# MLP down projections of a two-layer trunk kernel: activations as the stationary operand, weights as the moving one

## The chip, the cores and the metric

The kernel runs on one core of a Trainium2 chip. The metric is the time of one execution on the device in microseconds (us), as the median of several runs. The profile is one further execution, taken by the hardware profiler. PE is the matrix engine (TensorE), PEld its weight loads, DVE the vector engine, ACT the scalar engine, POOL GpSimd, and SP the queue from which the loads are issued.

## The reference

A trunk of two layers over 256 tokens with 2048 features, all in float32. Each layer has a mixing part (layer 0: an RWKV-7 recurrence, layer 1: attention with forget gates) and an MLP with 8192 hidden features:

```python
def rms_norm(x, gain):
    y = x * lax.rsqrt(jnp.mean(x * x, axis=-1, keepdims=True) + RMS_EPS)
    return y * gain

def squared_relu_mlp(h, w_up, w_down):
    return jnp.square(jax.nn.relu(h @ w_up)) @ w_down
...
for layer in range(DEPTH):            # DEPTH = 2
    x = x + mixed                     # RWKV-7 or attention
    x = x + squared_relu_mlp(rms_norm(x, ffn_norm[layer]), mlp_w_up[layer], mlp_w_down[layer])
return rms_norm(x, final_norm)
```

The change touches `squared_relu_mlp` alone, and in it the product with `w_down` (8192 x 2048 in each layer).

## The kernel before

**Layout.** The stream `xT` lies in SBUF with features on the partitions: 16 blocks (KT) of 128 features, each 128 x 256 tokens. Every float32 operand is kept as two parts, a rounded high part and the rest (`h` and `lo` of a weight, `[:, k, 0, :]` and `[:, k, 1, :]` of an activation in `opA` and `opB`), and a product is high x high + high x rest + rest x high.

**Weights.** `load_split` (line 194) loads a piece of a weight matrix into a raw buffer (`wr`) from SP. ACT casts it to the high part (`wh`, line 204), and DVE subtracts that from the raw piece (`wl`, line 206). In the MLP a raw piece is WK = 4 blocks of 128 rows by 512 columns (1024 KB), split two blocks at a time. The raw and split buffers have pools of their own there, three buffers of each kind (WRAW, WSP). Elsewhere pieces of 512 KB run through the global pool `wraw` with four buffers.

**The MLP.** `mlp` (line 346) goes through four chunks (c) of 2048 hidden features. In each chunk there are four up groups (g), each giving 512 hidden features, and four down groups, each adding to 512 features of `xT`. Both kinds of group use `gemm_wide` (line 241). For each of the 16 blocks k and each of the four 128-column parts of the weights, a part of the weight is stationary and the activations move. A 512-wide matmul (line 254) takes the high weight with both activation parts side by side, and a 256-wide one (line 256) takes the rest of the weight with the high activations. So one block takes eight matmuls, and the four PSUM banks of a group are taken in turn from two pools of four banks (`psm`, `pss`). At the end of a group ACT copies the second half of each bank (line 261) and DVE adds the first half to it (line 262).

**After a down group** DVE multiplies by `r2`, the square of the RMS factor (line 363, one value per token, laid along the free dimension), and POOL adds the result to `xT` (line 366; DVE for the last group of a layer). `r2` is made once in each layer, after the first up group: `norm.ln()` sums the squares over the partitions with matmuls against ones (`nps`, line 324) and takes the logarithm on ACT (line 326), and `norm.power` the exponential (line 330). In the last chunk `final` follows each pair of blocks: squares for the next norm and the operands of the next stage (`after0`, `after1`).

**Order.** The order in which each engine takes its instructions is settled when the program is built, and is not simply that of the code: casts and subtractions for coming pieces stand ahead of the evictions of a finished group.

The stage that computes the attention's values (lines 924 to 938) already has the form to which the change turns the down groups: activations stationary, 512 weight columns moving, two banks for the two halves of the tokens, and the factor per token as a scalar per partition. Ahead of it two transposes (line 922) turn that factor round.

## Time and profile before

| what | us |
|---|---|
| median of 3 runs | 2569.55 (2557.32 to 2569.76) |
| the profiled execution, its own time | 2563.87 |
| its span, first to last instruction | 2562.1 |

The span is what the profile's rows are measured in; 1.8 us of the profiled execution's time lie around it. A row of a group of instructions gives line, engine, operation, output<-inputs, count, busy time and mean duration of one; a row of the timeline gives the start, the duration and the instruction, and in brackets how long its engine had been idle and what ended that.

### The profile page before, as it was taken

The numbers are of one execution on the slowest core, as the hardware profiler recorded it, in microseconds if no ns is written. First come the engines' busy times: TensorE is split into PE (matmuls) and PEld (weight loads), VectorE is DVE, ScalarE is ACT, GpSimd is POOL, SyncE is SP. The second block draws the span as 40 slices with busy tenths as digits, with TensorE's granted clock in tenths as the row PEclk, the third lists the DMA queues.
The fourth block names the chain that finished last, engine by engine and source line by source line (L and its number), as shares of the span: only waits on it lengthen the run. The fifth ranks groups of instructions, "written<-read, shape, count | busy, mean of one in ns | idle before, by whom it ended". The sixth has DMA issues, their size and how long they took to land. (4 is left out here: it accounts for less than half of the span.)

```text
span 2562.1 us, 47095 instructions
## 1 busy us (share of the span) xinstructions
PE 2474.4 (97%) x19102; PEld 2208.3 (86%) x19102; DVE 1620.4 (63%) x2266; ACT 1272.2 (50%) x2098; POOL 526.2 (21%) x428
## 2 busy tenths in 40 slices
PE   6889999999999999999999999999999999999997
PEld 4889988888888888888888898999988888888886
DVE  8987557776755555555556655677555555555555
ACT  3655435454555454454455544455454454554454
POOL 5444324332311211111112100010011112111112
PEclk9999999999999999999999999999999999999998
DMA  4668856555765555555556366546455555556553
GB/s 149 199 201 246 249 180 189 161 166 159 237 202 189 182 181 197 182 189 188 181 181 197 97 183 196 181 158 198 149 190 184 194 187 191 183 195 194 186 195 116
DMA packets 279641, 472.88 MB, mean 185 GB/s; under 512 B 52464, under 2 KB 62976, under 8 KB 279424
## 3 DMA queue, kind: packets, MB, share of 16 engines
q1 hardware_dynamic: 279424, 469.89, 57.9%
q8 instruction: 149, 2.44, 0.4%
q14 instruction: 68, 0.56, 0.1%
HBM read 445.70 MB, written 24.13 MB: 183 GB/s over the span
## 5 line engine op out<-in xcount | busy, mean ns | idle before, releaser
L206 DVE TENSOR_TENSOR wl<-wr,wh 128x1024 fp32r<-128x1024 f32 (+1 forms) x960 | 965.9, 1010 | 740.9 <-ACT wh L204 735.7
L204 ACT CAST wh<-wr 128x1024 fp32r<-128x1024 f32 (+1 forms) x969 | 815.8, 846 | 909.7 <-PE mmw L254 595.0
L254 PE MATMUL mmw<-opB,wh 128*128 128x512 f32 x2048 | 717.4, 397 | 4.9 <-DVE xT L850 4.9
L254 PE MATMUL mmw<-opA,wh 128*128 128x512 f32 x2048 | 718.0, 397 | 0.2 <-ACT wh L204 0.2
L256 PE MATMUL mmw<-opA,wl 128*128 128x256 f32 x2048 | 572.5, 280 | 0.9 <-DVE wl L206 0.9
L256 PE MATMUL mmw<-opB,wl 128*128 128x256 f32 x2048 | 571.7, 279 | 0.0
L254 PEld LDWEIGHTS mmw<-opB,wh 128*128 128x128 f32 x2048 | 384.9, 188 | 97.4 <-DVE xT L850 5.1
L254 PEld LDWEIGHTS mmw<-opA,wh 128*128 128x128 f32 x2048 | 384.9, 188 | 93.0 <-ACT wh L204 0.5
L256 PEld LDWEIGHTS mmw<-opA,wl 128*128 128x128 f32 x2048 | 386.5, 189 | 1.4 <-DVE wl L206 1.3
L256 PEld LDWEIGHTS mmw<-opB,wl 128*128 128x128 f32 x2048 | 386.4, 189 | 0.2
L212 PE MATMUL mm<-opB,wh 128*128 128x256 f32 x1024 | 304.0, 297 | 1.2 <-DVE wh L202 1.2
L214 PE MATMUL mm<-opB,wl 128*128 128x256 f32 x1024 | 294.7, 288 | 7.0 <-DVE wl L206 4.8
L213 PE MATMUL mm<-opB,wh 128*128 128x256 f32 x1024 | 294.6, 288 | 3.9 <-DVE opB L343 3.8
L366 POOL TENSOR_TENSOR xT<-xT,mt 128x512 f32<-128x512 f32 x60 | 128.8, 2147 | 533.8 <-DVE mt L363 533.8
L212 PE MATMUL mm<-opA,wh 128*128 128x256 f32 x768 | 227.7, 297 | 0.0
L214 PE MATMUL mm<-opA,wl 128*128 128x256 f32 x768 | 218.5, 285 | 2.7 <-POOL wl L206 1.5
L213 PE MATMUL mm<-opA,wh 128*128 128x256 f32 x768 | 218.8, 285 | 0.0
L353 POOL TENSOR_TENSOR ms<-mt 128x512 f32<-128x512 f32 x64 | 81.1, 1267 | 636.5 <-ACT mt L351 636.5
L214 PEld LDWEIGHTS mm<-opB,wl 128*128 128x128 f32 x1024 | 198.4, 194 | 9.2 <-DVE wl L206 5.6
L213 PEld LDWEIGHTS mm<-opB,wh 128*128 128x128 f32 x1024 | 198.4, 194 | 7.5 <-DVE opB L343 5.7
L212 PEld LDWEIGHTS mm<-opB,wh 128*128 128x128 f32 x1024 | 198.2, 194 | 5.4 <-DVE wh L202 1.4
L214 PEld LDWEIGHTS mm<-opA,wl 128*128 128x128 f32 x768 | 147.5, 192 | 3.7 <-POOL wl L206 1.7
(252 smaller groups left out, 2711.0 us busy)
## 6 DMA issues: line engine op xcount, KB each, us to landing
wr<-in_mlp_w_up_dram SPq DMA_DIRECT2D x128, 1024.0 KB, 5.4
wr<-in_mlp_w_down_dram SPq DMA_DIRECT2D x128, 1024.0 KB, 5.0
wr<-in_w_rkv_dram SPq DMA_DIRECT2D x96, 512.0 KB, 4.7
wr<-in_w_kvf_dram SPq DMA_DIRECT2D x64, 512.0 KB, 3.7
wr<-in_w_o_dram SPq DMA_DIRECT2D x32, 512.0 KB, 4.0
wr<-in_fox_w_q_dram SPq DMA_DIRECT2D x32, 512.0 KB, 3.8
wr<-in_fox_w_o_dram SPq DMA_DIRECT2D x32, 512.0 KB, 4.0
s_bk<-bk SPq DMA_DIRECT2D x8, 512.0 KB, 3.0
```

Of the source, the lines that this page charges most:

```text
L204: nc.scalar.copy(h, raw[:, k:k + per, :])
L206: (G if share["l"] and c % share["l"] == 0 else V).tensor_tensor(lo, raw[:, k:k + per, :], h.bitcast(F32), op=ALU.subtract)
L212: mm(ps, wh, xh, start=first and bank_first, stop=False, skip_group_check=True)
L213: mm(ps, wh, xl, start=False, stop=False, skip_group_check=True)
L214: mm(ps, wl, xh, start=False, stop=last, skip_group_check=True)
L254: mm(ps[m], h[:, m * P:(m + 1) * P], x[:, k].rearrange("p h t -> p (h t)"), start=k == 0, stop=False, skip_group_check=True)
L256: mm(ps[m][:, 0:T], lo[:, m * P:(m + 1) * P], x[:, k, 0, :], start=False, stop=k == KT - 1, skip_group_check=True)
L353: G.tensor_tensor(s, t, t, op=ALU.mult)
L366: (V if end and g == 3 else G).tensor_tensor(xs, xs, t, op=ALU.add)
```

## The change

The up groups stay as they are, but load pieces of half the size (WK = 2, 512 KB). The MLP's own raw pools go; its pieces run through the global `wraw` (four buffers), and the split pools get four buffers in place of three.

The down groups are written anew (`down_group`). The weights move, 512 columns at a time, and a 128 x 128 part of the activations is stationary. For each block k there are three 512-wide matmuls into each of two banks, one bank for each half of the tokens; all 16 blocks of a group make 96 matmuls where there were 128. In the last piece of a group the first half of the tokens is finished ahead of the second. The result lies with tokens on the partitions. It is scaled by the factor per token and summed over the chunks in a new SBUF tile `y` (16 KB in a partition): by ACT in chunk 0, by one DVE instruction (`scalar_tensor_tensor`) that reads the bank, the factor and `y` in the later chunks. The copies, additions, multiplications and POOL's additions to `xT` at each group's end are gone.

For the factor, `r2` is transposed by two PE transposes (into `rps`) after the first up group, and a DVE copy takes one column for each half (`rc`).

In the last chunk `finish` turns a finished group of `y` back: eight 128 x 128 transposes into two banks, two DVE additions to `xT`, and `final` for the two pairs of blocks. It is called after the first piece of the next group, and for the fourth group after the loop: 32 transposes in each layer.

```diff
-WK, WRAW, WSP = 4, 3, 3
+WK, WSP = 2, 4
...
     def mlp(layer, norm, pool, wpools, a, b, final):
         r2 = None
+        y = pool.tile([P, 2, D], F32, tag="y", name="y", bufs=1)
+        late = []
+
+        def down_group(c, g):
+
+            pool_, tag = ((pss, "side"), (psm, "mm"))[g // 2]
+            ps = [pool_.tile([P, 512], F32, tag=tag, name="mmd") for _ in range(2)]
+            for k0 in range(0, KT, WK):
+                r0 = c * D + k0 * P
+                hl = load_split(w_down[layer, r0:r0 + WK * P, g * 512:g * 512 + 512]
+                                .rearrange("(k p) n -> p k n", p=P), P, WK, 512, 2, *wpools)
+                last = k0 + WK == KT
+                for i, kk in [(i, kk) for i in range(2) for kk in range(WK)] if last else \
+                        [(i, kk) for kk in range(WK) for i in range(2)]:
+                    k, t = k0 + kk, slice(i * P, (i + 1) * P)
+                    h, lo = hl[kk]
+                    mm(ps[i], b[:, k, 0, t], h, start=k == 0, stop=False)
+                    mm(ps[i], b[:, k, 1, t], h, start=False, stop=False)
+                    mm(ps[i], b[:, k, 0, t], lo, start=False, stop=k == KT - 1)
+                    if last and kk == WK - 1:
+                        yg = y[:, i, g * 512:g * 512 + 512]
+                        if c == 0:
+                            act(yg, ps[i], AF.Copy, scale=rc[:, i:i + 1])
+                        else:
+                            V.scalar_tensor_tensor(yg, ps[i], rc[:, i:i + 1], yg, op0=ALU.mult, op1=ALU.add)
+                if k0 == 0 and late:
+                    finish(late.pop())
+
+        def finish(g):
+
+            for j in range(2):
+                kp = 2 * g + j
+                tp = side("ytp").rearrange("p (k t) -> p k t", k=2)
+                for kk in range(2):
+                    for i in range(2):
+                        n = (2 * kp + kk) * P
+                        nc.tensor.transpose(tp[:, kk, i * P:(i + 1) * P], y[:, i, n:n + P], C("ident"))
+                xs = xT[:, 2 * kp:2 * kp + 2, :]
+                V.tensor_tensor(xs, tp, xs, op=ALU.add)
+                final(kp)
+
...
                 if r2 is None:
                     norm.ln()
                     r2 = norm.power(-1.0, "nr2")
+                    rps = side("rc")
+                    for i in range(2):
+                        nc.tensor.transpose(rps[:, i * P:(i + 1) * P], r2[:, i * P:(i + 1) * P], C("ident"))
+                    rc = pool.tile([P, 2], F32, tag="rc", name="rc", bufs=1)
+                    V.tensor_copy(rc, rps.rearrange("p (i n) -> p i n", n=P)[:, 0:2, 0])
             for g in range(4):
-                def down_evac(i, t, g=g, c=c):
-                    k = 4 * g + 2 * i
-                    V.tensor_tensor(t, t, bcast(r2, 2), op=ALU.mult)
-                    xs = xT[:, k:k + 2, :]
-                    end = c == FF // D - 1
-                    (V if end and g == 3 else G).tensor_tensor(xs, xs, t, op=ALU.add)
-                    if end:
-                        final(2 * g + i)
-                gemm_wide(w_down[layer, c * D:(c + 1) * D, :], g * 512, b, "mt", pool, wpools, down_evac)
+                down_group(c, g)
+                if c == FF // D - 1:
+                    late.append(g)
+        finish(late.pop())
...
-    with tc.tile_pool(name="mraw0", bufs=WRAW, reuse_waits="tile") as mr, \
-            tc.tile_pool(name="msp0", bufs=WSP, reuse_waits="tile") as ms, \
+    with tc.tile_pool(name="msp0", bufs=WSP, reuse_waits="tile") as ms, \
             tc.tile_pool(name="mlp0", bufs=2, reuse_waits="tile") as mp:
...
-        mlp(0, norm, mp, (mr, ms), opB, opA, after0)
+        mlp(0, norm, mp, (wraw, ms), opB, opA, after0)
...
-            tc.tile_pool(name="mraw1", bufs=WRAW, reuse_waits="tile") as mr, \
...
-        mlp(1, norm3, mp, (mr, ms), opA, opB, after1)
+        mlp(1, norm3, mp, (wraw, ms), opA, opB, after1)
```

Three places show how the instructions move. The first is on PE, in layer 0 at the end of the first up group, where the sum of squares (`nps`) stands; `rc` is the bank for the transposed factor, `nr` the factor itself. Before:

```order
L254 MATMUL mmw<-opB,wh 128x512
L256 MATMUL mmw<-opB,wl 128x256
L324 MATMUL nps<-nacc,ones 128x256 [waits Pool_49]
L324 MATMUL nps<-nacc,ones 128x256
L254 MATMUL mmw<-opB,wh 128x512 [waits Activation_49]
L256 MATMUL mmw<-opB,wl 128x256 [waits DVE_49]
```

The same place after the change:

```order
L254 MATMUL mmw<-opB,wh 128x512
L256 MATMUL mmw<-opB,wl 128x256
L324 MATMUL nps<-nacc,ones 128x256 [waits Pool_49]
L324 MATMUL nps<-nacc,ones 128x256
L403 MATMUL rc<-k_85,nr_11038 128x128 [waits Activation_49]
L403 MATMUL rc<-k_85,nr_11038 128x128
L254 MATMUL mmw<-opB,wh 128x512
L256 MATMUL mmw<-opB,wl 128x256 [waits DVE_49]
```

The two transposes of the factor stand directly behind the sum of squares, with a wait for ACT, and all matmuls of the second up group stand behind them.

The second place is on PE, in layer 0 where the first up group of a later chunk follows the last down group (`mmd` are the banks of a down group, `mmw` those of an up group). Before, the down group's last matmuls and the up group's first:

```order
L254 MATMUL mmw<-opA,wh 128x512
L256 MATMUL mmw<-opA,wl 128x256
L254 MATMUL mmw<-opB,wh 128x512 [waits Activation_49]
L256 MATMUL mmw<-opB,wl 128x256 [waits DVE_49]
L254 MATMUL mmw<-opB,wh 128x512 [waits PE_49]
L256 MATMUL mmw<-opB,wl 128x256
L254 MATMUL mmw<-opB,wh 128x512 [waits PE_49]
```

After:

```order
L364 MATMUL mmd<-wh,opA 128x512
L365 MATMUL mmd<-wh,opA 128x512
L366 MATMUL mmd<-wl,opA 128x512
L254 MATMUL mmw<-opB,wh 128x512 [waits Activation_49]
L256 MATMUL mmw<-opB,wl 128x256 [waits DVE_49]
L254 MATMUL mmw<-opB,wh 128x512
L256 MATMUL mmw<-opB,wl 128x256
L254 MATMUL mmw<-opB,wh 128x512 [waits DVE_49]
L256 MATMUL mmw<-opB,wl 128x256
L254 MATMUL mmw<-opB,wh 128x512 [waits DVE_49]
```

The down group's matmuls are all 512 wide, and the third and the fourth bank of the up group, which are those of the down group just finished, now wait for DVE.

The third place is on DVE, between two down groups of a later chunk. Before, the eviction of a group:

```order
L206 TENSOR_TENSOR wl<-wr,wh 128x1024 [waits PE_49,Activation_49]
L262 TENSOR_TENSOR mt<-mmw,mt 128x256 [waits Activation_49] x3
L363 TENSOR_TENSOR mt<-mt,nr_11032 128x512 [waits DVE_49]
L206 TENSOR_TENSOR wl<-wr,wh 128x1024 [waits DMAHW4_49,PE_49,Activation_49]
L262 TENSOR_TENSOR mt<-mmw,mt 128x256 [waits Activation_49]
L363 TENSOR_TENSOR mt<-mt,nr_11032 128x512 [waits DVE_49]
```

After:

```order
L206 TENSOR_TENSOR wl<-wr,wh 128x1024 [waits DMAHW4_49,PE_49,Activation_49]
L206 TENSOR_TENSOR wl<-wr,wh 128x1024 [waits DMAHW5_49,PE_49,Activation_49]
L206 TENSOR_TENSOR wl<-wr,wh 128x1024 [waits DMAHW6_49,PE_49,Activation_49]
L372 SCALAR_TENSOR_TENSOR y<-mmd,rc,y 128x512 [waits PE_49] x2
L206 TENSOR_TENSOR wl<-wr,wh 128x1024 [waits DMAHW7_49,Activation_49]
```

Two instructions take the place of six, and the subtractions for the first three pieces of the next group stand ahead of them.

## The prediction

> **What bounds the kernel now.** I read the profile's page first, for the engines' shares, then PE's waits, then windows of each layer's MLP.
>
> ```profile
> PE 2474.4 (97%) x19102; PEld 2208.3 (86%) x19102; DVE 1620.4 (63%) x2266; ACT 1272.2 (50%) x2098; POOL 526.2 (21%) x428
> PE mmw L254 <- DVE xT L850: 4.9, 1, 4.9
> 900.00:1300.00 400.00, 400.00 (x2266) 346.99 (x2265) 227.39 (x250) 191.13 (x253) 60.77 (x36) 1.00 0.57 185
> 1900.00:2300.00 400.00, 400.00 (x2309) 349.75 (x2308) 230.14 (x255) 195.29 (x259) 60.88 (x36) 1.00 0.59 190
> ```
>
> The window rows give length, busy time of PE, PEld, DVE, ACT and POOL, granted clock, DMA share and GB/s. In both MLPs PE has no idle time in 400 us, while DVE is busy for 57%, ACT for 48% and the DMA engines for under 60%. The longest wait of an MLP matmul is 4.9 us, once. So an MLP lasts as long as its stream of matmuls, and what leaves DVE, ACT and POOL is worth nothing by itself. What counts is the spacing of matmuls, and what the change puts into PE's queue.
>
> A busy share says nothing of spacing, so I take it from first and last starts. These rows cover the 512-wide matmuls of up groups in stretches of both layers; between their ends lie whole down groups too:
>
> ```profile
> L254 PE MATMUL mmw<-opB,wh x512: 394/399/404, 884.5 to 1155.5; 128*128 128x512 f32 x171
> L254 PE MATMUL mmw<-opA,wh x576: 392/394/396, 1900.4 to 2277.3; 128*128 128x512 f32 x192
> L933 PE MATMUL mmv<-wh,opB x128: 388/390/477, 1530.0 to 1616.5; 128*128 128x512 f32 x128
> ```
>
> In layer 0 the stretch holds 512 pairs (a 512-wide and a 256-wide matmul) of up groups and 256 of the down groups between: 271.0 us over 767 steps, **0.3533 us a pair**. In layer 1 it is 576 and 512: 376.9 over 1087, **0.3467 us**. The granted clock is 1.00 in both, so the same stream has two paces; what sets them the trace does not say. The third row is the value stage, which has the very form of the new down groups: 127 steps of three 512-wide matmuls in 86.5 us, **0.2270 us a matmul**, the joints of its groups included.
>
> **The change part by part.** All sums go against the profiled execution's own 2563.9 us. The median of the runs shown stands 5.7 us higher, and its runs spread over 12 us; a pace that holds for some groups in one execution and not in another could do that.
>
> *The stream.* An old group has 64 pairs: 64 x 0.3533 = 22.6 us in layer 0 and 64 x 0.3467 = 22.2 us in layer 1. A new down group has 96 matmuls: 96 x 0.2270 = 21.8 us. Over 16 down groups in each layer that is 16 x 0.82 + 16 x 0.40 = **19.5 us gained**. The columns streamed are the same, 3072 for each block; only two starts of eight are saved. The up groups keep either pace: here about half ran at the slower one. All at one or the other would move the sum by 16 x 0.43 = 7 us either way, and I keep half.
>
> *The transposes.* They are of a kind that attention has:
>
> ```profile
> 1646.59 0.49 PE L972 MATMUL ptp<-k,lg 128*128 128x128 f32 x3
> 1646.92 0.39 PE L951 MATMUL sp<-kT,qT 128*128 128x128 f32 x2
> L972 PE MATMUL ptp<-k,lg x48: 270/272/273, 1646.6 to 1763.2; 128*128 128x128 f32 x48
> ```
>
> Three occupy PE for 0.33 us before the next matmul starts, 0.11 each, though one lasts 272 ns from start to end. In each layer 24 of the 32 stand inside the stream: 48 x 0.11 = 5.2, with their joints **5.5 us lost**. Their input is ready: the eviction of a group ends about 1.5 us after its last matmul, and the transposes stand 12 matmuls (2.7 us) behind that. The last eight of a layer belong to its tail, below.
>
> The Trainium skill, page "TensorE: Matmul & The Clock Gate", Part 4: PE-mode transpose, speaks against this change: it gives about 275 ns for a transpose in a kernel's context, for bf16. By that figure the 48 would take 13.2 us, and the sum would be 8 us more; the trace has the same figure as the duration of one and 0.11 us as the spacing.
>
> *The factor for each token.* Here a wait is added.
>
> ```profile
> 725.17 1.02 PE L324 MATMUL nps<-nacc,ones 128*128 128x256 f32 x4
> 725.84 0.59 PE L254 MATMUL mmw<-opB,wh 128*128 128x512 f32 x1
> 728.53 0.62 ACT L342 CAST opA<-ms 128x512 fp32r<-128x512 f32 x1 [1.02 <-POOL ms L353]
> 729.05 0.41 ACT L330 ACTIVATE nr<-nln 128x256 f32<-128x256 f32 x1
> ```
>
> Today the second up group starts at 725.84, right behind the sum of squares, and the factor is ready at 729.46, behind evictions, a logarithm and a cast that waits for POOL; nobody on PE needs it then. Now two transposes of it stand ahead of the second up group, and 128 pairs queue behind them. The group would start at about 729.46 + 0.2 + 2 x 0.11 = 729.9, which is 4.0 us later; the casts that run ahead meanwhile shorten nothing, since PE is the bound. Twice: **8 us lost**. This could be nothing only if ACT took the exponential before the evictions, and its order is unchanged there.
>
> *The clock after such a gap.*
>
> ```profile
> 1792.10 0.39 PE L214 MATMUL mm<-opB,wl 128*128 128x256 f32 x1 [2.46 <-DVE wl L206]
> 1793.60:1796.90 3.30, 3.30 (x17) 3.30 (x16) 2.98 (x5) 1.12 (x2) 0.00 (x0) 0.50 0.96 335
> 694.50:697.80 3.30, 3.30 (x15) 3.18 (x16) 3.30 (x4) 2.71 (x6) 2.49 (x2) 0.50 0.70 199
> 1800.00:1820.00 20.00, 20.00 (x169) 20.00 (x169) 14.06 (x20) 11.11 (x20) 2.85 (x2) 1.00 0.52 171
> ```
>
> After an idle time of 2.46 us, and after the 4.9 us above, the granted clock was 0.50 for some 3.3 us. PE then started 15 to 17 matmuls where the full clock gives 3.3 x 8.45 = 28: 1.3 to 1.5 us lost. My two gaps of 4 us lie between, so **3 us lost**, with 0 as the other end.
>
> *Banks and evictions.*
>
> ```profile
> L937 DVE TENSOR_SCALAR vS<-mmv,rT x4: 750/751/752, 1552.1 to 1617.4; 128x512 f32<-128x512 f32 x4
> L206 DVE TENSOR_TENSOR wl<-wr,wh 128x1024 fp32r<-128x1024 f32 x512 | 629.5, 1230 | 551.8 <-ACT wh L204 551.7
> ```
>
> Where an up group follows a down group, its third and fourth bank are those just filled. The second half's eviction starts some 0.4 us after the group's last matmul has started, or behind a subtraction (1.23 us) and the first half's eviction. With 0.75 us for reading a bank it ends 1.2 to 1.8 us after that start, and PE wants the bank after 0.23 us and three pairs, 1.3 us. A chunk's start thus costs 0 to 0.8 us. There are six, the two after chunk 0 behind ACT, whose queue has a cast of 1 us between the halves: **3 us lost**, 0 to 5. A down group behind an up group takes the banks evicted first, and needs them when they come free: 0. Between down groups the banks alternate, and POOL's additions and the copies that go were hidden behind PE already: 0.
>
> *Loads.* Pieces of 512 KB through four buffers feed the value stage at the same need:
>
> ```profile
> 1532.00:1550.00 18.00, 18.00 (x81) 14.92 (x80) 0.00 (x0) 0.00 (x0) 1.00 0.64 194
> wr<-in_w_kvf_dram SPq DMA_DIRECT2D x64, 512.0 KB, 3.7
> ```
>
> There PE had no idle time, and a piece landed 3.7 us after its issue. SP issues 512 loads in place of 256 and has nothing else in its queue in the MLP. A buffer comes back some 2.4 us (cast and subtraction) after PE is done with the piece four earlier, and is needed 4 x 2.7 us after that point: 8.5 us for 3.7. I take 0, with that cover named.
>
> *Ends.* The additions to `xT` that close layer 1 end 3.7 us after the last matmul's start:
>
> ```profile
> 2543.74 0.28 PE L256 MATMUL mmw<-opB,wl 128*128 128x256 f32 x1
> 2546.77 0.69 DVE L366 TENSOR_TENSOR xT<-xT,mt 128x512 f32<-128x512 f32 x1
> 1417.78 0.39 PE L256 MATMUL mmw<-opA,wl 128*128 128x256 f32 x1 [0.95 <-DVE wl L206]
> ```
>
> The new chain is: end of the matmul 0.4, eviction 0.8, four transposes 0.5 and their end 0.2, with the sum of squares of earlier blocks between (1.0 today, beside it partly), two additions 1.4: 3.3 to 4.0. So 0, within 0.5 either way, in both layers. In layer 0's last group DVE is so full today that PE waits 0.95 us for a subtraction; with fewer evictions there that should go: **1 us gained**. The start of layer 0's MLP, where the 4.9 us stand, has DVE busy throughout before and after: 0, with 3 us gained as the other end, since that matmul now stands behind the output projection's.
>
> Sum: -19.5 + 5.5 + 8 + 3 + 3 - 1 = -1.0, so **2563 us**, 0.3% under the median shown. Differences under 0.5% can hardly be told from none here.
>
> **The rivals.**
>
> *All up groups at the quicker pace, and short waits.* It needs only that the new joints start the pairs as those in layer 1 were started: -7, less 3 of clock or banks: 2553, or a few us less. Against it: the slower pace held for nearly all of layer 0.
>
> *Transposes that do not overlap.* If each of the 64 took its 272 ns, they would cost 64 x 0.16 = 10 us more: 2573. The spacing of 0.11 speaks against it.
>
> *The new stream has a slower pace too.* The pair's two paces differ by 6.6 ns, 3.3 a matmul; over 3072 matmuls 10 us: 2573. The value stage showed one pace only, over 86 us.
>
> *The weights come late*: the case for slower. Four buffers of 512 KB hold 2 MB where three of 1 MB held 3. If a landing takes L, a piece takes the longer of 2.72 us and (L + 2.4)/4. It decides from L = 8.5 us. With L = 9.5 a down piece would take 2.98 us, 0.26 more on 256 pieces: 66 us slower, 2630. For it: the share of the DMA engines is 0.64 on average at this need. Against: a landing of 3.7 us.
>
> **How the numbers follow.** The cut at 0.5% under the median is 2556.7, that above it 2582.4. The forecast with its open terms (up groups' pace, clock, banks) fills 2557 to 2571: 0.66. The quick case: 0.16, about half of it under 2553. The two at 2573: 0.05 each. The weights late: 0.08. The range 2553 to 2574 leaves out some 0.08 below and 0.08 above. Faster 0.16, same 0.66 + 0.10 = 0.76, slower 0.08.
>
> **What would show it.** 512-wide matmuls of the down groups 0.227 us apart in both layers; transposes 0.11 us apart; an idle PE of nearly 4 us before L403 in each layer with a clock of 0.50 behind it; waits of a few tenths at the third and fourth bank of six up groups; no PE wait for a cast or subtraction inside a down group. I would be wrong if the new stream were spaced otherwise, if the factor came much earlier or later, or if many up groups changed their pace.

## The result, and the profile after

The changed kernel took 2570.99 us (median of 22 runs, 2561.79 to 2578.82), the kernel before 2559.34 us over as many runs (2545.40 to 2569.76). The ratio is **1.0043, with an interval of 1.0029 to 1.0058**: 0.4% slower, where 2563 us had been forecast, 0.3% under the median then shown and hardly to be told from no difference. The time itself lies inside the stated range of 2553 to 2574 us. The profiled execution of the changed kernel has a span of 2569.4 us, 7.3 more than that of before; the rest of the 11.7 us between the medians comes from the profiled execution of before, which lay 4.5 us above the median of its runs.

The shares and the longest waits of PE after the change (page and waits; a wait's three numbers are its sum, how often, the longest):

```profile
PE 2479.0 (96%) x18146; PEld 2171.5 (85%) x18146; DVE 1557.1 (61%) x2136; ACT 1243.3 (48%) x1986; POOL 402.6 (16%) x368
PE rc L403 <- ACT nr L330: 6.6, 2, 3.3
PE mmw L254 <- DVE xT L891: 6.2, 1, 6.2
```

PE executes 956 instructions fewer than before and is busy for 4.6 us more. One wait is new, that of the factor's transposes. No wait inside a group appears, and the weights are in time: within a down group nothing stands between the matmuls.

So the question is the spacing. The first matmul of each triple in three steady down groups (the second to the fourth of the first chunk), in layer 0 and in layer 1 (durations min/median/max in ns, then first and last start):

```profile
L364 PE MATMUL mmd<-wh,opA x96: 389/389/389, 823.2 to 887.8; 128*128 128x512 f32 x96
L364 PE MATMUL mmd<-wh,opB x96: 393/395/397, 1942.8 to 2009.3; 128*128 128x512 f32 x96
```

Between the starts lie 95 x 3 = 285 matmuls. Layer 0: 64.6 / 285 = **0.2267 us**, as foreseen. Layer 1: 66.5 / 285 = **0.2333 us**, in every one of its groups. A group of 96 takes 21.76 us in layer 0 and 22.40 in layer 1, where an old group took 22.19 in layer 1. There the new form is slower than the old one. The same thing shows in the duration of a single matmul, 389 ns against 395.

The seam behind the first up group of layer 0, on PE and on ACT (start, duration, instruction, and in brackets the idle time and what ended it):

```profile
727.24 0.28 PE L256 MATMUL mmw<-opB,wl 128*128 128x256 f32 x1
727.36 1.02 PE L324 MATMUL nps<-nacc,ones 128*128 128x256 f32 x4
731.71 0.44 PE L403 MATMUL rc<-k,nr 128*128 128x128 f32 x2 [3.32 <-ACT nr L330]
731.90 0.48 PE L254 MATMUL mmw<-opB,wh 128*128 128x512 f32 x1
...
730.72 0.62 ACT L342 CAST opA<-ms 128x512 fp32r<-128x512 f32 x1 [1.02 <-POOL ms L394]
731.24 0.41 ACT L330 ACTIVATE nr<-nln 128x256 f32<-128x256 f32 x1
```

From the sum of squares to the second up group it is 4.54 us, where it was 0.67 before (725.17 to 725.84). That is 3.9 us more, and in layer 1 it is 4.0. ACT takes the exponential behind a cast that itself waited for POOL, as before, but now PE's whole queue stands behind it. The clock behind the gap, in layer 0 and in layer 1 (window, length, busy times, granted clock, DMA share, GB/s):

```profile
731.90:735.20 3.30, 3.30 (x14) 2.77 (x14) 1.01 (x3) 0.89 (x2) 1.04 (x1) 0.59 0.29 110
1849.80:1853.10 3.30, 3.30 (x12) 2.82 (x11) 0.85 (x2) 0.71 (x2) 1.04 (x1) 0.50 0.28 105
1853.20:1858.00 4.80, 4.80 (x23) 4.10 (x23) 1.23 (x1) 1.05 (x1) 0.00 (x0) 0.76 0.00 0
732.50:735.90 3.40, 3.40 (x12) 2.82 (x12) 0.69 (x1) 0.62 (x1) 0.79 (x1) 0.50 0.11 42
1848.70:1855.40 6.70, 5.97 (x19) 5.17 (x20) 1.54 (x3) 2.15 (x5) 1.04 (x1) 0.50 0.27 76
```

The half clock lasts longer in layer 1 than in layer 0 after idle times of the same length: the last two rows are the whole of it, 3.4 us that begin behind the gap in layer 0, and 6.7 us that begin before the gap ends in layer 1. The page "TensorE: Matmul & The Clock Gate" of the Trainium skill, Part 1: The HAM clock gate, describes windows of about 3.4 us that run freely, and says that the moment at which the clock changes depends on where in a window the first matmul falls. One such window and two of them fit the two stretches of this trace.

The timeline of PE where the transposes stand between two pieces of a down group:

```profile
1357.28 0.40 PE L366 MATMUL mmd<-wl,opA 128*128 128x512 f32 x1
1357.51 1.03 PE L384 MATMUL ytp<-k,y 128*128 128x128 f32 x8
1358.30 0.47 PE L364 MATMUL mmd<-wh,opA 128*128 128x512 f32 x1
```

Eight take 0.79 us from the first start to the next matmul, 0.10 each. Of those who wait for a bank of the down groups, PE's weight loads for up groups have this row (sum, times):

```profile
  PEld mmw L254: 0.4, 2
```

The banks are free in time but for 0.4 us. Last, the stage between the MLPs: the last attention matmul, the first group of layer 1's MLP and the only wait of PE between them, in the kernel before:

```profile
L978 PE MATMUL op<-pt,vS x16: 270/273/275, 1708.4 to 1766.7; 128*128 128x128 f32 x16
L254 PE MATMUL mmw<-opA,wh x64: 394/398/404, 1832.3 to 1854.6; 128*128 128x512 f32 x64
PE mm L214 <- DVE wl L206: 3.0, 2, 2.5
```

And in the changed kernel, where no wait is left but 0.7 us at the MLP's first matmul:

```profile
L1018 PE MATMUL op<-pt,vS x16: 271/272/274, 1702.4 to 1760.7; 128*128 128x128 f32 x16
L254 PE MATMUL mmw<-opA,wh x64: 392/396/502, 1821.3 to 1844.7; 128*128 128x512 f32 x64
```

It took 1832.3 - 1766.7 = 65.6 us and takes 60.6: 5.0 us gained where I had looked for nothing. The wait for a subtraction ahead of the MLP, and the half clock behind it, are gone. In exchange the first group of layer 1 is 1.1 us longer (23.4 against 22.3 from first to last start).

### The profile page after: what moved, and what is told of

It reads as the page before. It is cut to its first block, busy times and chain, and to the rows that moved or that the text cites. A ratio compares the mean times of both kernels' runs of the same rounds, so it can differ in the third digit from the quotient of the medians.

```text
span 2569.4 us, 45510 instructions
## 1 busy us (share of the span) xinstructions
PE 2479.0 (96%) x18146; PEld 2171.5 (85%) x18146; DVE 1557.1 (61%) x2136; ACT 1243.3 (48%) x1986; POOL 402.6 (16%) x368
## 4 chain that ended last, share of the span: by engine, by line
PE 87%; DVE 6%; DMA 2%; ACT 2%; issue 2%; POOL 1%; SPq 0%; DVEq 0%; POOLq 0%; ACTq 0%
PE mmw L254 19%; PE mmw L256 9%; PE mmd L364 9%; PE mmd L366 9%; PE mmd L365 9%; PE mm L212 7%; PE mm L213 7%; PE mm L214 7%; DVE wl L206 2%; PE zyus L820 1%; PE i L649 1%; PE mmv L973 1%; PE mmv L974 1%; PE mmv L975 1%; DVE xs L489 1%
## 5 line engine op out<-in xcount | busy, mean ns | idle before, releaser
L254 PE MATMUL mmw<-opB,wh 128*128 128x512 f32 x1024 | 364.0, 400 | 6.2 <-DVE xT L891 6.2
L254 PE MATMUL mmw<-opA,wh 128*128 128x512 f32 x1024 | 363.3, 398 | 0.7 <-DVE xT L1053 0.7
L256 PE MATMUL mmw<-opA,wl 128*128 128x256 f32 x1024 | 288.8, 282 | 0.0
L256 PE MATMUL mmw<-opB,wl 128*128 128x256 f32 x1024 | 288.6, 282 | 0.0
L254 PEld LDWEIGHTS mmw<-opB,wh 128*128 128x128 f32 x1024 | 193.9, 189 | 53.4 <-DVE xT L891 6.5
L254 PEld LDWEIGHTS mmw<-opA,wh 128*128 128x128 f32 x1024 | 193.5, 189 | 48.3 <-DVE xT L1053 1.3
L364 PE MATMUL mmd<-wh,opB 128*128 128x512 f32 x512 | 202.9, 396 | 0.0
L366 PE MATMUL mmd<-wl,opB 128*128 128x512 f32 x512 | 202.2, 395 | 0.0
L365 PE MATMUL mmd<-wh,opB 128*128 128x512 f32 x512 | 202.2, 395 | 0.0
L364 PE MATMUL mmd<-wh,opA 128*128 128x512 f32 x512 | 199.9, 391 | 0.0
```

The source lines that it names most:

```text
L254: mm(ps[m], h[:, m * P:(m + 1) * P], x[:, k].rearrange("p h t -> p (h t)"), start=k == 0, stop=False, skip_group_check=True)
L256: mm(ps[m][:, 0:T], lo[:, m * P:(m + 1) * P], x[:, k, 0, :], start=False, stop=k == KT - 1, skip_group_check=True)
L364: mm(ps[i], b[:, k, 0, t], h, start=k == 0, stop=False)
L365: mm(ps[i], b[:, k, 1, t], h, start=False, stop=False)
L366: mm(ps[i], b[:, k, 0, t], lo, start=False, stop=k == KT - 1)
```

## The experiments

Each ratio is to the kernel before, run beside the kernel in question on the same chip. From chip to chip the median of the kernel before lay between 2551 and 2564 us, so times of different experiments are better compared by their ratios.

**1. The same kernel again; two offsets exchanged.** The split weights of the two layers lie differently in SBUF: in the build their first addresses are 164896 (32 more than a multiple of 64) in layer 0 and 193600 (a multiple of 64) in layer 1. The 32 bytes come from `rc`, whose pool opens ahead of the split pool in layer 1 and behind it in layer 0. The run `after_again` has no edit.

> The changed kernel, unaltered, for a second trace. In the first one a down group's 96 matmuls took 21.76 us in layer 0 and 22.40 us in layer 1, in all sixteen groups of each. Theory address (what the moving weights' place in SBUF decides: the split weights of layer 0 begin 32 bytes behind a multiple of 64, those of layer 1 on a multiple of 64): again 21.8 in layer 0 and 22.4 in layer 1. Theory chance (a pace that a stall happens to set and that then holds, as the up groups seem to have): the layers may change places, or one layer show both paces. The up groups, with 22.61 or 22.19 us: by either theory they may come out otherwise than in the first trace (24 of 32 at the slower pace).

`swap_offsets` moves both by 32 bytes:

```diff
+            tc.tile_pool(name="pad0", bufs=1, reuse_waits="tile") as pp, \
             tc.tile_pool(name="msp0", bufs=WSP, reuse_waits="tile") as ms, \
...
+        pad = pp.tile([P, 8], F32, name="pad")
+        G.memset(pad, 0.0)
...
-                    rc = pool.tile([P, 2], F32, tag="rc", name="rc", bufs=1)
+                    rc = pool.tile([P, 16], F32, tag="rc", name="rc", bufs=1)
...
```

> The split weights of layer 0 are moved up by 32 bytes, to a multiple of 64, by a small tile ahead of them, and those of layer 1 by 32 bytes off a multiple of 64, by a wider tile rc. Nothing else changes. Theory address: the paces change places, layer 0's down groups 22.40 us and layer 1's 21.76, and the time stays within 0.3% of the changed kernel's (ratio to the kernel before about 1.004). Theory chance: down groups as before the swap (21.76 and 22.40), or a mix that has nothing to do with the offsets. The wait for the factor, 3.9 and 4.0 us more of idle PE, stays in both.

The repeated kernel took 2573.85 us in its one run. Its down groups were again 21.76 us in layer 0 and 22.40 in layer 1, all of them, while its up groups came out otherwise: chunks 0 and 2 of layer 0 and chunk 3 of layer 1 at 22.19 us, the rest at 22.61. The swapped kernel took 2574.70 us (ratio 1.0068, 1.0039 to 1.0097). Its down groups, rows as above:

```profile
L364 PE MATMUL mmd<-wh,opA x96: 393/395/397, 822.4 to 888.9; 128*128 128x512 f32 x96
L364 PE MATMUL mmd<-wh,opB x96: 388/388/388, 1951.7 to 2016.9; 128*128 128x512 f32 x96
```

Layer 0 is now the slow one (66.5 us), with the numbers that layer 1 had. Layer 1 is quicker (65.2), though not as quick as layer 0 had been (64.6). So the place decides and chance does not, but not simply by whether it is a multiple of 64.

**2. The factor later.** The transposes and the copy go from behind the first up group to behind the third:

```diff
+                if c == 0 and g == 2:
                     rps = side("rc")
                     for i in range(2):
                         nc.tensor.transpose(rps[:, i * P:(i + 1) * P], r2[:, i * P:(i + 1) * P], C("ident"))
```

> The two transposes of the factor and the copy stand behind the third up group of chunk 0 instead of the first. Theory factor: the idle PE in front of them (4.65 and 4.80 us between the first group's last matmul and the next group's first, against 0.80 before the change) falls to under 1 us in both layers, the second group of each layer takes 22.2 to 23.0 us instead of 24.22 and 25.25, and the time falls by 3.9 + 4.0 + 1.6 + 2.3 = 11 to 12 us, to about 2559, a ratio to the kernel before of 1.000. Rival: the half clock behind the gap or the evictions hide most of it already, and the time falls by under 5 us (ratio over 1.002).

It took 2560.51 us (ratio 1.0009, 0.9981 to 1.0038). The timeline of PE at the old and at the new place:

```profile
722.80 1.02 PE L324 MATMUL nps<-nacc,ones 128*128 128x256 f32 x4
723.47 0.58 PE L254 MATMUL mmw<-opB,wh 128*128 128x512 f32 x1
...
768.29 0.38 PE L404 MATMUL rc<-k,nr 128*128 128x128 f32 x2
768.42 0.48 PE L254 MATMUL mmw<-opB,wh 128*128 128x512 f32 x1
```

And a window of this kernel in the second group:

```profile
731.90:735.20 3.30, 3.30 (x21) 2.93 (x20) 1.23 (x1) 1.17 (x2) 0.00 (x0) 1.00 0.80 250
```

No gap is left and the clock stays at 1.00; the two transposes take 0.13 us up to the next matmul's start. The ratios of this kernel and of the changed one differ by 0.0034 (8.7 us), their medians (of different chips) by 10.5 us, where 11 to 12 had been worked out. The intervals of the two ratios are too wide to exclude the rival's under 5 us. The traces exclude it: from the first matmul of the MLP to that of its third up group this kernel takes 7.2 us less in layer 0 and 7.3 us less in layer 1.

**3. The loads alone.** The kernel before with `WK, WSP = 2, 4` and `wraw` in place of its own raw pools, the down groups as they were.

> The kernel before with the change's loads alone: pieces of 512 KB through the common raw pool, four split buffers, the down groups as they were. Theory stream: loads are worth nothing, ratio 1.000 within 0.002, groups of 22.19 or 22.61 us as in the kernel before. Rival loads: the smaller pieces bring waits of PE on casts and subtractions inside the groups, 5 us or more in all, ratio over 1.002.

Its ratio is 0.9981 (0.9952 to 1.0010). No wait appeared inside the groups. From the last attention matmul to the MLP of layer 1 it took 60.6 us, as in the changed kernel (1753.7 to 1814.3), and the waits at the end of layer 0's MLP were gone as well. So these two small gains belong to the loads, though the ratio alone can't tell this kernel from the one before. From the third group of each layer on its groups took 22.19 us in layer 0 and 22.61 in layer 1, the opposite of the profiled execution of before.

**4. Which place?** Four kernels on the late factor. In the first two only the split weights move (`rc` of 32 floats; a `pad` of 24 ahead of `msp0` and `rc` of 24), in the others the activations too. The "rest" in what follows is a first address modulo 128 bytes. The cut is from `operands_0_64`; `operands_96_0` has 16 and 8 floats in place of 24 and 16:

```diff
+    padA = big.tile([P, 24], F32, name="padA")
     opA = big.tile([P, KT, 2, T], F32R, name="opA")
+    padB = big.tile([P, 16], F32, name="padB")
     opB = big.tile([P, KT, 2, T], F32R, name="opB")
```

> Late factor, and layer 1's split weights moved from rest 64 to rest 32 (their first address modulo 128 bytes) by a rc of 128 bytes; layer 0's have rest 32 already. So far rest 32 gave 21.76 us a down group (layer 0), rest 64 22.40 (layer 1, and layer 0 in the swap), rest 96 21.97 (layer 1 in the swap). Theory rest: layer 1's down groups at 21.76 us, 16 x 0.64 = 10 us off the late factor's time, about 2550, ratio to the kernel before 0.997. Theory layer (the stationary operand, opB in layer 1, adds 0.2 us by itself): layer 1 at 21.97, 7 us off, about 2553.5. Theory chance: 22.40 in layer 1 or paces that change from group to group.

> Late factor, with the split weights of both layers at rest 0 modulo 128 bytes. Theory 64 (a multiple of 64 bytes is what is slow): 22.40 us a down group in both layers. Theory rest: both layers alike, at a value of their own, between 21.76 and 22.40 or outside. Theory layer: layer 1 slower than layer 0 by 0.2 us at the same rest.

> Late factor, split weights of both layers at rest 32, and the activations opA moved from rest 32 to rest 0, opB from 32 to 64. The up groups stream opB in layer 0 and opA in layer 1; the down groups have opA stationary in layer 0 and opB in layer 1. Theory rest holds for the up groups too: their two paces (22.19 and 22.61 us, changing with the execution) turn into one pace a layer, other in layer 0 (rest 64) than in layer 1 (rest 0). Theory two paces: both still occur, whatever the rest. The down groups stay at 21.76 in both layers if the stationary operand's place counts for nothing; else they change.

> As the run before, with opA at rest 96 and opB at rest 0. Theory rest: layer 0's up groups show here what layer 1's show at rest 0 in the run before, and layer 1's a pace for rest 96. Theory two paces: 22.19 and 22.61 again, mixed. Down groups 21.76 in both layers if the stationary operand's place counts for nothing.

Times: `offset_32` 2559.73 us (ratio 0.9980, 0.9963 to 0.9997), `offset_0` 2561.62 in one run, `operands_0_64` 2564.71 (1.0019, 0.9998 to 1.0040), `operands_96_0` 2565.31 in one run. Three steady down groups of layer 1 in `offset_32`:

```profile
L364 PE MATMUL mmd<-wh,opB x96: 390/393/404, 1928.8 to 1995.0; 128*128 128x512 f32 x96
```

In both layers of `offset_0`:

```profile
L364 PE MATMUL mmd<-wh,opA x96: 394/394/394, 818.6 to 885.1; 128*128 128x512 f32 x96
L364 PE MATMUL mmd<-wh,opB x96: 392/392/392, 1936.5 to 2003.0; 128*128 128x512 f32 x96
```

None of the theories written down for `offset_32` holds: at rest 32 layer 1 takes 66.2 us, neither 64.6 nor 65.2 nor the old 66.5. `offset_0` comes out as a slow multiple of 64 would have it. In both layers of `operands_0_64`, down groups and then three up groups (192 pairs between the starts):

```profile
L368 PE MATMUL mmd<-wh,opA x96: 392/397/400, 816.9 to 883.7; 128*128 128x512 f32 x96
L368 PE MATMUL mmd<-wh,opB x96: 399/399/399, 1936.7 to 2003.2; 128*128 128x512 f32 x96
L258 PE MATMUL mmw<-opB,wh x193: 391/391/392, 906.4 to 972.9; 128*128 128x512 f32 x193
L258 PE MATMUL mmw<-opA,wh x193: 392/394/394, 2205.5 to 2272.7; 128*128 128x512 f32 x193
```

In both layers of `operands_96_0`, down groups and then up groups of layer 1:

```profile
L368 PE MATMUL mmd<-wh,opA x96: 394/394/394, 816.3 to 881.6; 128*128 128x512 f32 x96
L368 PE MATMUL mmd<-wh,opB x96: 393/395/397, 1934.8 to 2001.3; 128*128 128x512 f32 x96
L258 PE MATMUL mmw<-opA,wh x193: 397/397/398, 2204.6 to 2272.4; 128*128 128x512 f32 x193
```

In these two kernels the split weights have rest 32 in both layers, and four places of the activations give 66.8, 66.5, 65.3 and 66.5 us. So the stationary operand's place counts too. The up groups of `operands_0_64` show one pace in each layer, as the theory of the rest has it; but those of layer 0 in `operands_96_0`, which stream activations of rest 0, show 22.19 and 22.61 and not the 22.40 seen at rest 0 before. What orders all these rows is the **difference** of the two first addresses, modulo 256 bytes: the D of the expectations below. The three rows of up groups have D = 96, 160 and 64, and 66.5, 67.2 and 67.8 us. At D = 96 all steady up groups of a layer had the quick pace, in these kernels three times.

**5. The difference put to the test.** `same_difference` moves everything from `opA` on up by 32 bytes and layer 1's split weights by 224 more, so that in the MLPs all addresses are multiples of 64 and D is 0 in both layers. `offset_192_224` tries two more values. `best_offsets` gives each kind of group its own D, and `before_offset_96` moves the split weights of the kernel before (`pad` of 24 floats in both layers). The core of `best_offsets`:

```diff
-            h = wsp.tile([p, per, n], F32R, tag="wh", name="wh")
+            h = wsp.tile([p, per * n + pad], F32R, tag="wh", name="wh")[:, at:at + per * n].rearrange(
+                "p (k n) -> p k n", k=per)
...
-                            *wpools)
+                            *wpools, 64, 24)
...
-                                .rearrange("(k p) n -> p k n", p=P), P, WK, 512, 2, *wpools)
+                                .rearrange("(k p) n -> p k n", p=P), P, WK, 512, 2, *wpools, 64, 0)
```

> Difference D: the first address of the split weights less that of the activations of the same matmuls, modulo 256. In the traces so far the down groups took 21.76 us at D = 0, 22.40 at 32 and 96, 21.97 at 64, 22.31 at 128, 22.49 at 160, in either layer. Here, on the late factor, everything is moved up by 32 bytes, and layer 1's split weights by 224 more: all first addresses are multiples of 64, and D is 0 for all groups of both layers. Theory difference: 21.76 us a down group in both layers, layer 1 for the first time. Theory rest (the split weights or the activations on a multiple of 64 are slow by themselves): 22.40 in both. The up groups have D = 0 as before the change: 22.19 or 22.61, changing.

> Late factor; split buffers 256 bytes longer, in which the pieces of up groups begin at 96 bytes and those of down groups at 0; layer 1's split weights moved so that D is 96 for all up groups (22.19 us in all 45 full groups seen at 96) and 0 for all down groups. Theory difference: up groups 22.2, down groups 21.76 in both layers; against the late factor's traced run (2555.5 span, 29 up groups at 22.6, layer 1's down groups at 22.4) 29 x 0.42 + 16 x 0.64 = 22 us less, a span of about 2533, ratio to the kernel before 0.990 to 0.993. Theory rest or chance: up groups at mixed paces and no gain beyond the late factor's 1.000.

> Late factor, layer 0's split weights at D = 192 for up and down groups, layer 1's at D = 224. Theory difference: one pace in each layer for the down groups, at 192 like the other multiples of 64 (21.8 to 22.3), at 224 like the odd multiples of 32 (22.4 to 22.5). Theory rest: 22.40 in layer 1, whose split weights stand on a multiple of 64 less 0, 21.8 to 22.0 in layer 0.

> The kernel before with its split weights moved up by 96 bytes in both layers, so that D goes from 0 to 96 for all groups. Nothing else changes. Theory difference: all 64 groups of both layers at 22.19 us; against the traced run before (30 groups at 22.61 in layer 0) 13 us less, and against the median of the runs before some 7 us: ratio 0.997. It is then the change's fair rival: late factor with best offsets should still be 64 - 64 x ... shorter by 32 x 0.43 less 48 transposes of 0.11, 8 us. Theory chance: a mix of 22.19 and 22.61, ratio 1.000.

`same_difference` took 2543.37 us in one run, `offset_192_224` 2569.68 in one. `best_offsets` took 2540.15 (ratio **0.9947**, 0.9925 to 0.9969), `before_offset_96` 2548.87 (0.9975, 0.9954 to 0.9996). Down groups of `same_difference` in both layers:

```profile
L366 PE MATMUL mmd<-wh,opA x96: 389/389/390, 818.0 to 882.6; 128*128 128x512 f32 x96
L366 PE MATMUL mmd<-wh,opB x96: 388/389/390, 1926.0 to 1990.6; 128*128 128x512 f32 x96
```

64.6 us in both layers at D = 0, on addresses that are multiples of 64: the rest is refuted, the difference holds. Down groups of `offset_192_224`, D = 192 and 224:

```profile
L364 PE MATMUL mmd<-wh,opA x96: 393/394/395, 821.3 to 887.8; 128*128 128x512 f32 x96
L364 PE MATMUL mmd<-wh,opB x96: 395/396/397, 1944.6 to 2011.1; 128*128 128x512 f32 x96
```

66.5 us or 22.40 a group at both. At 224 that was expected, at 192 it lies outside the 21.8 to 22.3 foreseen: the values between follow no rule that I had. Up and down groups of `best_offsets` in both layers:

```profile
L256 PE MATMUL mmw<-opB,wh x193: 390/392/393, 902.2 to 968.8; 128*128 128x512 f32 x193
L256 PE MATMUL mmw<-opA,wh x193: 390/392/393, 2186.4 to 2253.0; 128*128 128x512 f32 x193
L366 PE MATMUL mmd<-wh,opA x96: 388/389/390, 815.0 to 879.5; 128*128 128x512 f32 x96
L366 PE MATMUL mmd<-wh,opB x96: 388/389/390, 1923.1 to 1987.7; 128*128 128x512 f32 x96
```

Everything at its quick pace: 66.6 us for three up groups, 64.5 and 64.6 for three down groups. The ratio lies above the 0.990 to 0.993 expected. The span was 2537.0 us, where about 2533 had been worked out; against the late factor's trace the MLP of layer 0 began 0.7 us later, and the first groups of the two layers were 1.6 and 0.9 us longer. In `before_offset_96` all groups from the third of each layer on took 22.19 us, but for the last two of layer 0 with their waits. All traces together, one group in us:

| D | down group | up group |
|---|---|---|
| 0 | 21.76 (12 layers) | 22.19 or 22.61, changing |
| 32 | 22.40 (5) | 22.19 or 22.61, changing |
| 64 | 21.97 (2) | 22.61 (2) |
| 96 | 22.40 (3) | 22.19 (11) |
| 128 | 22.31 (1) | 22.47 (1) |
| 160 | 22.49 (1) | 22.40 (1) |
| 192 | 22.40 (1) | 22.61 (1) |
| 224 | 22.40 (1) | 22.19 (1) |

Behind each value stands in how many layers of the traces, experiment 6 included, all steady groups had it. Old down groups, which have the form of up groups, count among these where they stand at the same D. For up groups at 64 and 192 the one pace rests on eight and four chunks. In `factor_late`, at D = 0 and 32, all up groups of chunks 1 to 3 of both layers had 22.61 us too, so those two values may be changing ones as well.

The value stage is one more test, in a part of the kernel that was not moved for it. Its split weights stay at 39968, but `padA` and `padB` move `opB` by 32, 160 and 96 bytes in `same_difference`, `operands_0_64` and `operands_96_0`. So its D is 224, 96 and 160 there, and 0 in all other kernels. The first matmul of each triple in the changed kernel, then in these three in that order:

```profile
L973 PE MATMUL mmv<-wh,opB x128: 389/389/481, 1524.0 to 1610.4; 128*128 128x512 f32 x128
L976 PE MATMUL mmv<-wh,opB x128: 394/396/476, 1515.2 to 1604.2; 128*128 128x512 f32 x128
L981 PE MATMUL mmv<-wh,opB x128: 399/399/479, 1523.1 to 1612.1; 128*128 128x512 f32 x128
L981 PE MATMUL mmv<-wh,opB x128: 391/397/481, 1520.1 to 1609.5; 128*128 128x512 f32 x128
```

From first to last start it takes 86.4 us at D = 0, and 89.0, 89.0 and 89.4 in the three. With four groups of 96 matmuls the table gives 86.4 + 4 x 0.64 = 89.0 at 224 and 96, and 86.4 + 4 x 0.73 = 89.3 at 160. The stage follows the down groups.

**6. Does it make up the miss, and what is the form worth?** `after_d0` is the changed kernel with a `rc` of 64 floats and nothing else. `small_offset_96` has the loads of experiment 3 and D = 96. `best_again` is `best_offsets` once more.

> The changed kernel with a rc of 256 bytes in place of 32, which moves layer 1's split weights from D = 32 to D = 0; the factor stays early. Theory difference: layer 1's down groups 21.76 us as layer 0's, 16 x 0.64 = 10 us less than the changed kernel, about 2561, a ratio to the kernel before of 1.000 within 0.002: the place where the prediction was (no difference that can be told). The waits for the factor stay at 3.3 us of idle PE in both layers. Rival: the stall's half clock or the up groups' pace moves with it, and the ratio stays above 1.003.

> The kernel before with the change's loads (pieces of 512 KB, common raw pool, four split buffers) and D = 96 for all groups: the old form without its address cost and without the larger loads. All 64 groups at 22.19 us; against D = 96 alone (ratio 0.9975) some 5 us less, from the wait ahead of layer 1's MLP and the stall in layer 0's last group: ratio 0.995 to 0.996. Theory stream: the turned form (best_again) is still 3 to 6 us shorter: 32 x 0.43 less 48 transposes of 0.11 and the joints. Rival: nothing is left between the two within 2 us, and the gain of the best offsets was loads and addresses alone.

> Late factor and best offsets once more, beside the run before on one chip: ratio 0.993 to 0.996, up groups 22.19 and down groups 21.76 us in both layers, 3 to 6 us below small_offset_96 by theory stream, within 2 us of it by the rival.

`after_d0` took 2557.36 us (ratio 0.9988, 0.9961 to 1.0015). The down groups of layer 1:

```profile
L364 PE MATMUL mmd<-wh,opB x96: 389/389/389, 1934.6 to 1999.2; 128*128 128x512 f32 x96
```

And PE's wait for the factor in its layer 1:

```profile
PE rc L403 <- ACT nr L330: 3.3, 1, 3.3
```

64.6 us: with 224 bytes more in one tile the changed kernel can't be told from the one before, though the factor's wait is still paid twice. The profiled execution is 18.7 us shorter than that of the changed kernel. Layer 1's down groups are 10.2 us of it. Most of the rest is the changing pace of the up groups (8 slow ones where there were 20) and a shorter half clock in layer 1; whether the edit has a part in these is not shown. On the same chip `small_offset_96` took 2546.92 us (0.9938, 0.9913 to 0.9963) and `best_again` 2538.63 (0.9920, 0.9890 to 0.9951). The 512-wide matmuls of up groups of layer 1 in `small_offset_96`, with old down groups between them:

```profile
L254 PE MATMUL mmw<-opA,wh x570: 391/392/392, 1893.7 to 2268.4; 128*128 128x512 f32 x190
```

So with like loads and each at the best offset seen, the turned groups are 8.3 us shorter than the old ones. The profiled executions agree: from the first matmul of layer 0's MLP to the end it is 1849.9 us in `small_offset_96` and 1841.9 in `best_again`, 8.0 less. (Their spans differ by more, since the MLP began 8.4 us later in the first.) That is more than the 3 to 6 expected, and what 32 x 0.43 = 13.8 less 5.5 for the transposes gives. The runs of `best_again` also lie within 5.7 us of one another, those of the kernel before on that chip within 34.0. A pace of the groups that changes from run to run would fit this; no run shows it by itself.

## Why the prediction missed

| step of the prediction | predicted | profiled executions |
|---|---|---|
| down groups' stream, layer 0 | -13.1 | 16 x (21.76 - 22.61) = -13.6 |
| down groups' stream, layer 1 | -6.4 | 16 x (22.40 - 22.19) = **+3.4** |
| up groups' pace | 0 | 4 quicker, 10 slower by 0.43: +2.6 |
| 48 transposes | +5.5 | 6 groups longer by 0.9: +5.4 |
| wait for the factor | +8 | 3.9 + 4.0 = +7.9 |
| half clock behind it | +3 | second groups longer by 1.2 and 2.6: +3.8 |
| banks and evictions | +3 | +0.4 |
| waits in layer 0's last group | -1 | 0.9 + 0.2 of before gone: -1.1 |
| stage ahead of layer 1's MLP | none | -5.0 |
| first groups, and a later start of layer 0's MLP | 0 | 1.1 + 0.5 + 1.7 = +3.3 |
| sum | -1.0 | +7.1 of 7.3 |

**The step that failed** is the first: "A new down group has 96 matmuls: 96 x 0.2270 = 21.8 us", applied to "16 down groups in each layer". The row of the value stage was read rightly, and layer 0 ran at it. But that row belongs to one pair of addresses: the value stage's split weights (39968) and `opB` (93216) differ by a multiple of 256, D = 0, and so do those of layer 0's down groups. Layer 1's stood at D = 32, because the change's own 8-byte tile `rc` took 32 bytes ahead of them. This cost 9.8 us against the forecast, more than the whole miss of 8.2 on the profiled execution. Experiments 1, 4 and 5 show that the place decides. In three of their kernels the value stage itself took 89.0 to 89.4 us, so its row would have read otherwise there. `after_d0` shows that moving this one place takes the kernel from slower back to no difference, and that these groups are 10.2 us of it in the profiled executions.

The rival "the new stream has a slower pace too" had the right size (6.7 ns a matmul over the 1536 of one layer is 10 us) and 0.05. I set it aside because the value stage "showed one pace only". One pace at one place in memory was no evidence for another place.

**What held.** The wait for the factor was right in place, cause and size. So was the spacing of the transposes: 0.10 to 0.11 us is what they cost, and one lasts 272 ns. The figure of about 275 ns for bf16 in the Trainium skill, page "TensorE: Matmul & The Clock Gate", Part 4: PE-mode transpose, is again the duration here and not the spacing. The weights did not come late. The half clock was somewhat dearer than its middle value; of the 2.6 us in layer 1 some 0.4 is the slower pace of that chunk.

**What was mis-sized.** The banks were free in time: 0.4 us of waits for 3. The loads were costed at nothing and gained 5 us ahead of layer 1's MLP, which experiment 3 shows by themselves. The row of the 2.46 us was in the prediction, as evidence on the clock; I did not ask what put that wait there. The up groups' pace was left at half and half and went against the kernel in the profiled execution: 10 more slow groups in layer 1, 4 fewer in layer 0. With the 3.3 us of the first groups and the later start, which I had put at nothing too, these misses nearly cancel: 2.6 and 3.3 us on one side, 5.0 and 2.6 on the other. That is luck; without the 5.0 us ahead of layer 1's MLP the time would have been about 2576 us, outside the range.

**The base.** The forecast was made against one profiled execution, which lay 4.5 us above the median of the later runs. With it the forecast read as a small gain against the median shown; against the median of 22 runs the same number is 3.7 us slower.

## What to carry to other kernels

A spacing read from one stage holds for the addresses of that stage. Where PE is the bound over thousands of matmuls, compare the first addresses of the stationary and the moving operand before and after a change, even when a change only adds a tile of 8 bytes, and look at the spacing, from the first and the last start of many: here the steps were 2 to 8 ns a matmul. The duration of a single matmul is the poorer sign: at the one spacing of 0.2333 us, rows of down groups showed medians of 392 to 399 ns. And a result that only a scalar per token needs should not be waited for at the head of PE's queue: two transposes moved by two groups were worth about as much here as the whole turn of the down groups.

## What the runs showed of the hardware

The spacing of float32 matmuls whose operands stream without a wait, at a granted clock of 1.00, takes several values that are constant over a layer: 0.2267 to 0.2344 us for 512 columns with a new stationary part for each. D decides which, in the down groups of both layers and in the value stage, with two values at some D for pairs of a 512-wide and a 256-wide matmul. At D = 0 and 32 the same build showed either from chunk to chunk; what sets it there stays open.

The page "SBUF — State Buffer" of the Trainium skill, SBUF: two separate sides, says that PE never waits on anyone for its ports, and in its section on the bandwidth-pool intuition gives the weight loads a second read port that is independent. No run here tests the first. On the second, moving only where weights lie relative to activations changed the spacing by 2.9% (21.76 to 22.40 us a group), which two wholly independent ports would not lead one to expect. Whether it is the load of the next stationary part that meets the moving stream was argued from D alone and not shown; no run took the weight loads away. So whether the page is wrong here stays open.
